# A convolutional FFN taken apart into two phases, its down-projection done as seven products

## The chip, the core and the metric

The kernel runs on one core of a Trainium2 chip. It computes one whole decoder layer in one launch. The metric is the device time of one execution in microseconds (us), as the median of several runs; lower is better. The engines are named as in the profile: PE does the matmuls (PEld loads their weights), DVE, ACT and POOL do the elementwise work, SP issues most of the DMAs. PE writes its results into eight PSUM banks of 128x512 numbers; everything else in the kernel's pools lies in SBUF.

## The reference, cut to what matters

Of the layer only its last part is touched: a gated feed-forward network with a causal convolution of width 3 over the tokens, on 1024 tokens, 1024 model columns and `D_FF` = 2816 hidden columns.

```
def conv_ffn(h, w_up, conv_w, conv_b, w_down):
    a, b = jnp.split(h @ w_up, 2, axis=-1)
    a = lax.conv_general_dilated(a, conv_w..., padding=[(CONV_WIDTH - 1, 0)], feature_group_count=D_FF) + conv_b
    return (jax.nn.gelu(a) * b) @ w_down
...
        x = x + merged @ w_o[l]
        x = x + conv_ffn(rms_norm(x, norm2_g[l]), w_up[l], conv_w[l], conv_b[l], w_down[l])
    return rms_norm(x, final_g)
```

## The kernel before, in words

Every product of two float32 numbers is made from three matmuls (`mm3`, L280 to L285): each operand is split into a high part `hi` that the PE's format holds and a low part `lo` = operand - `hi`, and hi·hi, hi·lo and lo·hi are added in PSUM. So an operand costs a cast on ACT, a subtraction on POOL or DVE, and three matmuls wherever it is used.

The 2816 hidden columns are handled as `NF` = 22 blocks of 128. The residual `x1`, 1024 tokens by 1024 columns, stays in SBUF, and the normalised input of the FFN lies there as seven prepared operands `B` (`B11`, `B21`, `B22` and the sums `T1` to `T4`, split into `hi` and `lo`, printed as `blk`).

`ffn` (L1357) is a generator that is entered twice. The first entry, in the middle of the output projection, loads and prepares the four operands of block 0. The second does the rest. For each block `j`:

- **Up-projection.** The two slices of `w_up` (for `a` and for `b`, each 1024x128, 512 KB) come in by two DMAs (L1370) into raw buffers (`wr` and `fr`, a ring of three). From them `prep` (L1374) makes the seven left operands of a seven-product scheme (Winograd's form of Strassen), `PRODUCTS`: the sums S1 to S4 on POOL (L1387 to L1394), the cast on ACT (L1398), the low part on POOL (L1399). `prep` is called three products ahead. A product is 4 x 3 = 12 matmuls of 128x512, into one PSUM bank, and is read out by ACT (L1500) or DVE (L1498, an add). Block 0 has eight products in four plus two groups, block 1 takes its seven in another order (`EARLY`).
- **Gate.** `conv` (L1437) and `gated` (L1452): the convolution of `a` over the tokens, gelu, times `b`, and the split of the gated activations of the first and second half of the tokens into `hi` and `lo`.
- **Down-projection of block j-1.** The rows of `w_down` of that block come in by two DMAs of 256 KB (L1404) and are split (`prep_down`, L1406 on ACT, L1407 on POOL). Then `down` (L1410) makes 16 tiles, 8 of tokens by 2 halves of the output columns, 3 matmuls each, into the PSUM bank printed as `T`, and DVE adds each to `x1` (L1419). They stand between the products: two or three tiles behind each.

After the loop the last two blocks' down-projections are made together, 16 tiles of 6 matmuls, and behind each pair of tiles the final normalisation of a tile of tokens: `squares` (L1547, ACT) and `finish` (L1553, DVE and POOL, and two stores to `out` of 256 KB, L1565).

The order on each engine is that of the program text, apart from what the scheduler of the framework moves; each engine goes through its instructions in order and waits for the semaphores of each, and SP also issues DMAs in order. An order is shown below with the change.

Of the kernel before, what the change touches and what calls it, by code (L numbers as in the profile page):

```python
# [13 lines left out]
P = 128  # L14
S = 1024
# [215 lines left out]
class Trunk:  # L231
# [1125 lines left out]
    def ffn(self, np_, x1, B):  # L1357
        nc, a, wp = self.nc, self.a, self.wp
        wup, wdn = a["w_up"][0], a["w_down"][0]
        raws, ops, wds, gs = {}, {}, {}, {}  # L1360
        cnt = {"raw": 0, "op": 0}
        last = NF - 1

        def load(j):
            pair = []
            for c0 in (j * P, DFF + j * P):
                pool, tag = (fp, "fr") if cnt["raw"] % 3 == 2 else (wp, "wr")
                cnt["raw"] += 1
                r = pool.tile([P, 8, P], F32, tag)
                nc.sync.dma_start(r, wup[:, c0:c0 + P].rearrange("(k p) n -> p k n", p=P))  # L1370
                pair.append(r)
            q = {"A11": pair[0][:, 0:4], "A12": pair[0][:, 4:8], "A21": pair[1][:, 0:4], "A22": pair[1][:, 4:8]}
            raws[j] = q

        def prep(j, i):

            if j > last:
                return
            if i == 0 and 0 < j < last:
                load(j + 1)  # L1380
            q = raws[j]
            name = (("A11", "A12", "A21", "A22") if j == 0 else [x for x, _ in (self.EARLY if j == 1 else self.PRODUCTS)])[i]
            g = nc.gpsimd.tensor_tensor
            e = g if j > 1 else nc.vector.tensor_tensor
            if name == ("S1" if j == 1 else "S2"):
# [13 lines left out]
            g(o[:, 1], q[name], o[:, 0].bitcast(F32), ALU.subtract)  # L1399
            ops[j, i] = o  # L1400

        def prep_down(j, n):
            raw = np_.tile([P, 512], F32, "tt")
            nc.sync.dma_start(raw, wdn[j * P:(j + 1) * P, n * 512:n * 512 + 512])  # L1404
            w = np_.tile([P, 2, 512], F32R, "t2") if j < last else wp.tile([P, 2, 512], F32R, ("wh", "wl")[n])
            nc.scalar.copy(w[:, 0], raw)  # L1406
            nc.gpsimd.tensor_tensor(w[:, 1], raw, w[:, 0].bitcast(F32), ALU.subtract)  # L1407
            wds[j, n] = w

        def down(j, t, n, tag="T"):  # L1410
            gh, gl = gs[j][t // 4]
            ts = slice((t % 4) * P, (t % 4) * P + P)
            ps = self.psA.tile([P, 512], F32, tag)
            if j == last:
                h0, l0 = gs[j - 1][t // 4]
                self.mm3(ps, (h0[:, ts], l0[:, ts]), (wds[j - 1, n][:, 0], wds[j - 1, n][:, 1]), True, False)
            self.mm3(ps, (gh[:, ts], gl[:, ts]), (wds[j, n][:, 0], wds[j, n][:, 1]), j != last, True)
            cs = slice(n * 512, n * 512 + 512)
            nc.vector.tensor_tensor(x1[:, t, cs], ps, x1[:, t, cs], ALU.add)  # L1419

        load(0)
        seq = [(0, i) for i in range(4)] + [(j, i) for j in range(1, NF) for i in range(7)]
# [3 lines left out]
        fp = Pool(self, "ffn", {"t1": 2, "sv": 2, "fst": 4})  # L1426
        load(1)
        AHEAD = 3
        todo = []
        for j in range(NF):  # L1430
            cw = [self.ccols[:, x * NF + j:x * NF + j + 1] for x in range(4)]
            sv = fp.tile([P, 2], F32, "sv")
            p1 = fp.tile([P, 512], F32, "p1")
            u2 = fp.tile([P, 512], F32, "u2")
            u3 = fp.tile([P, 512], F32, "u3")
            gs[j] = []

            def conv(hh, src):
                t1 = fp.tile([P, 512], F32, "t1")
                nc.scalar.activation(t1, src, AF.Identity, scale=cw[2], bias=cw[3])  # L1440
                for sh in (1, 2):
                    nc.vector.scalar_tensor_tensor(t1[:, sh:512], src[:, 0:512 - sh], cw[2 - sh], t1[:, sh:512],  # L1442
                                                   ALU.mult, ALU.add)
                if hh == 0:
                    nc.vector.tensor_copy(sv, src[:, 510:512])
                else:
                    nc.vector.scalar_tensor_tensor(t1[:, 0:1], sv[:, 1:2], cw[1], t1[:, 0:1], ALU.mult, ALU.add)
                    nc.vector.scalar_tensor_tensor(t1[:, 0:2], sv, cw[0], t1[:, 0:2], ALU.mult, ALU.add)
                nc.scalar.activation(t1, t1, AF.Gelu_apprx_tanh)
                gs[j].append(t1)  # L1450

            def gated(hh, b):  # L1452
                t1 = gs[j][hh]
                pool, tag = (wp, "wr") if (j, hh) == (last, 1) else (np_, ("x", "x", "gb")[(2 * j + hh) % 3])
                g = pool.tile([P, 2, 512], F32R, tag)
                gh, gl = g[:, 0], g[:, 1]
                nc.vector.tensor_tensor(t1, t1, b, ALU.mult)
                nc.scalar.copy(gh, t1)
                nc.vector.tensor_tensor(gl, t1, gh.bitcast(F32), ALU.subtract)
                gs[j][hh] = (gh, gl)  # L1460

            if j == 0:
                su = fp.tile([P, 512], F32, "su")
                for gi, grp in enumerate(((("A11", "B11"),), (("A12", "B21"),), (("A21", "B11"),), (("A22", "B21"),),
                                         (("A11", "T1"), ("A12", "B22")), (("A21", "T1"), ("A22", "B22")))):
                    ps = self.psA.tile([P, 512], F32, ("dn", "S", "S", "dn", "S")[gi % 5])
# [5 lines left out]
                    if gi % 2 == 0 and gi < 4:  # L1472
                        nc.scalar.copy((p1, u2)[gi // 2], ps)
                        continue
                    d, s = ((u3, p1), (su, u2), (p1, p1), (u2, u2))[(0, 0, 0, 1, 2, 3)[gi]]
# [223 lines left out]
```

## Time and profile before

| | |
|---|---|
| median of 3 runs | 1813.07 us (1812.57 to 1818.72) |
| the profiled execution | 1815.99 us, its span 1814.2 us, mean granted PE clock 0.985 |
| busy, share of the span | PE 96%, PEld 79%, DVE 68%, ACT 41%, POOL 32% |
| HBM read, written | 146.86 MB, 48.64 MB |

The stages by the times at which their instructions run: projections and the three attention mixers to about 880 us, merge 905 to 1008, output projection 1009 to 1108, FFN matmuls 1113 to 1803, and the last normalisation to the end of the span. The profile is of one execution: "span" is from its first to its last instruction, and its own time is a little longer. A row of the timeline has the start, the duration, the engine, the line, the operation and the tiles, and in brackets how long the engine had been idle and what ended that. A row of windows has for each engine the busy time and the count of instructions in a stretch of time, then the granted PE clock, the DMA engines' share and GB/s.

### The profile page before, as it was taken

The page shows a single profiled execution, that of the slowest core. Times are in us where ns is not written, and L with a number is a line of the kernel's source. Part 1 is how long each engine was busy: PE and PEld are TensorE (multiplying, and loading weights), DVE is VectorE, ACT ScalarE, POOL GpSimd, SP SyncE. Part 2 cuts the span into 40 slices and gives each one's busy share as a digit, 9 for nine tenths or more (in the row PEclk, how much of TensorE's full clock was granted, in tenths as well). Part 3 has the DMA queues.
Part 4 walks back from the last instruction along what each step waited for, and adds up shares of the span by engine and source line. Part 5 has one row for each costly group of instructions (what it writes and reads, how often), then busy time and mean ns, then how long its engine had stood idle before and what let it go on. Part 6 is the DMA issues. An engine that isn't in the chain of part 4 may idle for free.

```text
span 1814.2 us, 24514 instructions
## 1 busy us (share of the span) xinstructions
PE 1737.0 (96%) x8732; PEld 1425.5 (79%) x8732; DVE 1231.5 (68%) x2659; ACT 746.6 (41%) x1557; POOL 579.8 (32%) x435
## 2 busy tenths in 40 slices
PE   7999999879899999999999999899999999999997
PEld 6887887768687888888877887678878777877776
DVE  7366677646467775666567349877777777777777
ACT  5334555533354544555554224433333233333334
POOL 4311101002111111111134305555555555555561
PEclk9999999989899999999999999899999999999999
DMA  8756566677525264311466600121111111111112
GB/s 254 211 137 162 140 166 165 174 202 183 134 74 143 78 159 119 89 59 52 140 205 197 209 0 18 41 64 41 54 52 53 53 53 53 53 47 53 52 36 110
DMA packets 191648, 194.39 MB, mean 107 GB/s; under 512 B 16200, under 2 KB 155566, under 8 KB 191318
## 3 DMA queue, kind: packets, MB, share of 16 engines
q1 hardware_dynamic: 182870, 174.84, 34.3%
q10 hardware_dynamic: 8208, 15.21, 2.3%
q0 software_dynamic: 448, 2.78, 0.5%
q8 instruction: 69, 1.13, 0.3%
q14 instruction: 53, 0.43, 0.1%
HBM read 146.86 MB, written 48.64 MB: 108 GB/s over the span
## 4 chain that ended last, share of the span: by engine, by line
PE 52%; DVE 5%; DMA 2%; POOL 1%; ACT 1%; issue 1%; DVEq 0%; SPq 0%; ACTq 0%; POOLq 0%
PE dn L285 7%; PE dn L283 7%; PE dn L284 7%; PE S L285 5%; PE S L283 5%; PE S L284 5%; PE T L283 4%; PE T L285 4%; PE T L284 4%; PE T L769 1%; DVE t L1442 1%; DVE x L1419 1%; PE S L701 1%; PE PV L799 1%; DMA wr<-w_o 1%
## 5 line engine op out<-in xcount | busy, mean ns | idle before, releaser
L271 POOL TENSOR_TENSOR wl<-wr,wh 128x1024 fp32r<-128x1024 f32 (+2 forms) x60 | 113.4, 1890 | 696.6 <-ACT wh L269 605.5
L283 PE MATMUL dn<-hTh,wh 128*128 128x512 f32 x704 | 285.9, 406 | 2.0 <-DVE sl L488 2.0
L285 PE MATMUL dn<-hTh,wl 128*128 128x512 f32 x704 | 278.3, 395 | 0.0
L284 PE MATMUL dn<-hTl,wh 128*128 128x512 f32 x704 | 277.6, 394 | 0.0
L1419 DVE TENSOR_TENSOR x<-T,x 128x512 f32<-128x512 f32 x326 | 221.3, 686 | 9.9 <-PE T L285 9.4
L712 ACT ACTIVATE p<-S,sm 128x384 f32<-128x384 f32 (+2 forms) x192 | 106.5, 559 | 138.7 <-DVE sm L708 103.1
L285 PEld LDWEIGHTS dn<-hTh,wl 128*128 128x128 f32 x704 | 133.4, 190 | 29.2
L283 PEld LDWEIGHTS dn<-hTh,wh 128*128 128x128 f32 x704 | 134.3, 191 | 20.8 <-DVE sl L488 2.4
L284 PEld LDWEIGHTS dn<-hTl,wh 128*128 128x128 f32 x704 | 134.1, 191 | 19.1
L776 DVE TENSOR_TENSOR tl<-T,th 128x512 fp32r<-128x512 f32 (+2 forms) x202 | 115.4, 585 | 33.3 <-ACT th L775 32.3
L704 DVE TENSOR_REDUCE sm<-S 128x1 f32<-128x384 f32 (+2 forms) x192 | 96.3, 525 | 54.5 <-PE S L701 53.3
L775 ACT CAST th<-T 128x512 fp32r<-128x512 f32 (+2 forms) x202 | 99.7, 510 | 66.5 <-PE T L769 64.1
L701 PE MATMUL S<-k,q 114*128 114x384 f32 (+6 forms) x240 | 95.9, 400 | 16.0 <-issue 8.0
L798 PE MATMUL PV<-th,v 128*128 128x256 f32 (+1 forms) x362 | 93.9, 284 | 3.4 <-DVE yt L815 2.9
L769 PE MATMUL T<-ident,p 128*128 128x128 f32 x610 | 93.4, 275 | 2.1 <-DVE tl L776 2.1
L799 PE MATMUL PV<-tl,v 128*128 128x256 f32 (+1 forms) x362 | 89.2, 283 | 2.3 <-DVE tl L776 2.3
L283 PE MATMUL T<-t,x 128*128 128x512 f32 x219 | 89.9, 410 | 0.8 <-DVE x L1419 0.6
L697 PE MATMUL S<-k,q 128*128 128x384 f32 (+2 forms) x240 | 84.3, 351 | 6.5 <-DMA k<-dk_b 4.9
L285 PE MATMUL T<-t,x 128*128 128x512 f32 x219 | 86.2, 394 | 0.0
L284 PE MATMUL T<-t,x 128*128 128x512 f32 x219 | 85.6, 391 | 0.0
L769 PEld LDWEIGHTS T<-ident,p 128*128 128x128 f32 x610 | 72.6, 141 | 14.6 <-DVE tl L776 3.1
L798 PEld LDWEIGHTS PV<-th,v 128*128 128x128 f32 x362 | 69.1, 191 | 8.6 <-DVE yt L815 5.2
(481 smaller groups left out, 4494.1 us busy)
## 6 DMA issues: line engine op xcount, KB each, us to landing
wr<-w_in SPq DMA_DIRECT2D x44, 512.0 KB
wr<-w_up SPq DMA_DIRECT2D x30, 512.0 KB
dg<-f ACTq DMA_DIRECT2D x48, 256.0 KB
gr<-dg SPq DMA_DIRECT2D x24, 512.0 KB
tt<-w_down SPq DMA_DIRECT2D x44, 256.0 KB
x<-x SPq DMA_DIRECT2D x16, 512.0 KB
fr<-w_up SPq DMA_DIRECT2D x14, 512.0 KB
q<-dq_c SPq DMA_DIRECT2D x12, 512.0 KB
```

Source lines behind the costliest of these rows:

```text
L271: eng.tensor_tensor(lo, raw, hi.bitcast(F32), ALU.subtract)
L283: nc.tensor.matmul(out, st[0], mv[0], start=first, stop=False)
L284: nc.tensor.matmul(out, st[0], mv[1], start=False, stop=False)
L285: nc.tensor.matmul(out, st[1], mv[0], start=False, stop=last)
L701: nc.tensor.matmul(ps[:, 0:wn * P], q[1][0:R, qs], k[1][0:R, cs], start=False, stop=True)
L712: nc.scalar.activation(pt[:, 0:m, :].rearrange("p a b -> p (a b)"), v, AF.Exp, bias=mx, accum_out=sm[:, 2 + ci:3 + ci])
L769: nc.tensor.transpose(ps[:, n * P:(n + 1) * P], b, self.ident)
L775: nc.scalar.copy(th[:, cs], ps[:, cs])
L776: nc.vector.tensor_tensor(tl[:, cs], ps[:, cs], th[:, cs].bitcast(F32), ALU.subtract)
L798: nc.tensor.matmul(unit.pv[:, oc], w, th[:, cs], start=first and i == 0, stop=False)
L799: nc.tensor.matmul(unit.pv[:, oc], w, tl[:, cs], start=False, stop=e)
L1419: nc.vector.tensor_tensor(x1[:, t, cs], ps, x1[:, t, cs], ALU.add)
```

## The change

The FFN becomes two phases, with DRAM between them.

**Phase 1** makes only the up-projections and gates. The blocks are taken in the order 0, 11, 1, 12, ..., 10, 21. The gated activations are not split; as soon as the two blocks k and k+11 are there, they are the left operands of a second seven-product scheme: `sums` makes their four sums on DVE, and seven tiles of 256 KB are stored to DRAM (`dl[k]`). In the same phase `down_weights(k)` loads the two matching row blocks of `w_down` (512 KB each), makes the four sums T1 to T4 on POOL and stores them to DRAM (`dt[k]`, 2 x 512 KB); it is called in every second block. The low parts of the up-projection's operands (from the third block on) move from POOL to DVE. The convolution of the second half of the tokens reads its two halo columns from a buffer of 514 columns, which takes the place of two small fix-up instructions. The products rotate over all eight PSUM banks.

**Phase 2**, `ffn_down`, multiplies halves of the tokens (2 x 512), of the contraction (2 x 11 blocks) and of the outputs (2 x 512) in seven products. Six of them go over 11 operand pairs each: load the left and the right tile (two DMAs of 256 KB), one cast on ACT and one subtraction on DVE of 128x1024, then 4 tiles of tokens x 3 matmuls of 128x512, accumulated over the 11 pairs in four PSUM banks. The operands have a ring of five buffers and are asked for four ahead. The seventh product's eleven operands are prepared during the first six, one at every sixth step, and kept. The results are added to `x1` and to two helper sums `U` and `V`, and the last normalisation of the first four token tiles stands behind the fifth product, that of the other four behind each tile of the seventh.

The core of the diff (the block loop's bookkeeping and block 1's own order are left out):

```diff
+    DOWN = (("A11", "B11"), ("A12", "B21"), ("S2", "T2"), ("S1", "T1"), ("S4", "B22"), ("S3", "T3"), ("A22", "T4"))
...
+        order = [j for k in range(NH) for j in (k, k + NH)]
...
-            g(o[:, 1], q[name], o[:, 0].bitcast(F32), ALU.subtract)
-        def prep_down(j, n):
...
-        def down(j, t, n, tag="T"):
...
+            (v if s > 1 else g)(o[:, 1], q[name], o[:, 0].bitcast(F32), ALU.subtract)
+        def down_weights(k):
+            w = [np_.tile([P, 2, 512], F32, "t2") for _ in range(2)]
+            for x in range(2):
+                r = (k + x * NH) * P
+                nc.sync.dma_start(w[x], wdn[r:r + P].rearrange("p (n c) -> p n c", n=2))
+            g(w[0][:, 1], w[0][:, 1], w[0][:, 0], ALU.subtract)
+            g(w[1][:, 1], w[1][:, 1], w[0][:, 1], ALU.subtract)
+            g(w[0][:, 0], w[1][:, 1], w[0][:, 0], ALU.subtract)
+            g(w[1][:, 0], w[1][:, 0], w[1][:, 1], ALU.subtract)
+            for x in range(2):
+                nc.sync.dma_start(dt[k][:, 2 * x:2 * x + 2], w[x])
+        def left(k, name, src):
+            nc.sync.dma_start(dl[k][:, self.LEFT.index(name)], src)
+        def sums(k):
+            ga, gb = gs[k], gs[k + NH]
+            s1 = np_.tile([P, 512], F32, "tt")
+            v(s1, ga[:, 1], gb[:, 1], ALU.add)
+            left(k, "S1", s1)
+            v(ga[:, 1], ga[:, 0], ga[:, 1], ALU.subtract)
+            v(ga[:, 0], s1, ga[:, 0], ALU.subtract)
+            nc.sync.dma_start(dl[k][:, 0:2], ga)
+            v(gb[:, 0], gb[:, 0], ga[:, 0], ALU.subtract)
+            left(k, "S4", gb[:, 0])
...
+                if s > 1 and s % 2 == 0 and i == 2:
+                    sums(s // 2 - 1)
+                if s % 2 == 1 and i == 4:
+                    down_weights(s // 2)
+                ps = self.bank_tile()
...
-                for _ in range((0, 0, 0, 0, 5, 5, 6)[i] if j == 1 else ((i + 1) * 16) // 7 - (i * 16) // 7):
-                    if todo and j < last:
-                        down(*todo.pop(0))
...
+        def operands(p, k, keep=None):
+            an, bn = self.DOWN[p]
+            pool = ring()
+            raw = pool.tile([P, 2, 512], F32, "wr")
+            nc.sync.dma_start(raw[:, 0], dl[k][:, self.LEFT.index(an)])
...
+            nc.sync.dma_start(raw[:, 1], src)
+            hi, lo = ((keep or pool).tile([P, 2, 512], F32R, n) for n in (("hi", "lo") if keep else ("wh", "wl")))
+            nc.scalar.copy(hi, raw)
+            v(lo, raw, hi.bitcast(F32), ALU.subtract)
+            return hi, lo
+        def step(ps, op, t, first, last):
+            (hi, lo), ts = op, slice(t * P, t * P + P)
+            self.mm3(ps, (hi[:, 0, ts], lo[:, 0, ts]), (hi[:, 1], lo[:, 1]), first, last)
...
+        for p in range(6):
+            ps = [self.bank_tile() for _ in range(4)]
+            for k in range(NH):
+                n = p * NH + k
+                if n + AHEAD < len(seq):
+                    ops[n + AHEAD] = operands(*seq[n + AHEAD])
+                if n % 6 == 5:
+                    lasts.append(operands(6, len(lasts), rp))
+                o = ops.pop(n)
+                for t in range(4):
+                    step(ps[t], o, t, k == 0, k == NH - 1)
```

The orders below list instructions as line, operation, result and inputs, with the line numbers of the kernel that they come from; the numbers behind a tile's name tell buffers apart.

On POOL, early in phase 1. Before, a block's rows are the up-projection's sums (L1387 to L1394), its low parts (L1399) and the two low parts of `w_down` (L1407, `t<-tt`):

```order
L1394 TENSOR_TENSOR wr_12824<-wr_12824 128x512
L1399 TENSOR_TENSOR wh_13187<-wr_12826,wh_13187 128x512
L1407 TENSOR_TENSOR t_2636_13219<-tt_13217,t_2636_13219 128x512
L1399 TENSOR_TENSOR wl_13214<-wr_12826,wl_13214 128x512
L1399 TENSOR_TENSOR wh_13246<-su_13103,wh_13246 128x512
L1387 TENSOR_TENSOR su_13347<-wr_13070 128x512
L1389 TENSOR_TENSOR wr_13070<-fr_13068,wr_13070 128x512
L1399 TENSOR_TENSOR wl_13280<-wr_12824,wl_13280 128x512
L1399 TENSOR_TENSOR wh_13316<-fr_13068,wh_13316 128x512
L1391 TENSOR_TENSOR fr_13068<-su_13347,fr_13068 128x512
```

After, the four sums of `down_weights` (L1421 to L1424, one pair of `w_down` row blocks to each four rows), here of the eighth and ninth pair, and behind them the up-projection's sums of the seventh block (L1400 to L1407):

```order
L1421 TENSOR_TENSOR t_2778_14250<-t_2778_14250 128x512
L1422 TENSOR_TENSOR t_2779_14251<-t_2779_14251,t_2778_14250 128x512
L1423 TENSOR_TENSOR t_2778_14250<-t_2779_14251,t_2778_14250 128x512
L1424 TENSOR_TENSOR t_2779_14251<-t_2779_14251 128x512
L1421 TENSOR_TENSOR t_2827_14563<-t_2827_14563 128x512
L1422 TENSOR_TENSOR t_2828_14564<-t_2828_14564,t_2827_14563 128x512
L1423 TENSOR_TENSOR t_2827_14563<-t_2828_14564,t_2827_14563 128x512
L1424 TENSOR_TENSOR t_2828_14564<-t_2828_14564 128x512
L1400 TENSOR_TENSOR su_12711<-wr_12533 128x512
L1402 TENSOR_TENSOR wr_12533<-wr_12531,wr_12533 128x512
L1404 TENSOR_TENSOR wr_12531<-su_12711,wr_12531 128x512
L1407 TENSOR_TENSOR wr_12531<-wr_12531 128x512
```

The low parts have left POOL, and the scheduler has moved the sums of `w_down` forward: the program text calls the eighth pair in the sixteenth block, and it stands ahead of the seventh block's own sums. Each pair goes through the same two buffers `t2`, so its load waits until the pair before it is stored.

On DVE, in the middle of the block loop. Before, between the read-outs (L1498), the gate's products (L1457, L1459) and the convolution (L1442), stand the adds into the residual (L1419):

```order
L1498 TENSOR_TENSOR u_2809_14162<-dn_14259,u_2808_14161 128x512
L1419 TENSOR_TENSOR x_2293_11019<-T_14273,x_2293_11019 128x512
L1419 TENSOR_TENSOR x_2293_11019<-T_14278,x_2293_11019 128x512
L1419 TENSOR_TENSOR x_2293_11019<-T_14283,x_2293_11019 128x512
L1498 TENSOR_TENSOR p_2807_14160<-S_14295,u_2809_14162 128x512
L1419 TENSOR_TENSOR x_2293_11019<-T_14313,x_2293_11019 128x512
L1457 TENSOR_TENSOR t_2822_14239<-t_2822_14239,p_2807_14160 128x512
L1419 TENSOR_TENSOR x_2293_11019<-T_14318,x_2293_11019 128x512
L1459 TENSOR_TENSOR gb_14309<-t_2822_14239,gb_14309 128x512
```

After, the low parts of the up-projection's operands (L1412) stand between the read-outs (L1516), the convolution (L1470) and the gate (L1475):

```order
L1516 TENSOR_TENSOR u_2642_13385<-dn_13456,u_2641_13384 128x512
L1412 TENSOR_TENSOR wh_13474<-wr_13304,wh_13474 128x512
L1516 TENSOR_TENSOR p_2640_13383<-S_13477,u_2642_13385 128x512
L1475 TENSOR_TENSOR x_13386<-t_2651_13446,p_2640_13383 128x512
L1412 TENSOR_TENSOR wl_13497<-wr_13304,wl_13497 128x512
L1516 TENSOR_TENSOR u_2641_13384<-T_13500,u_2641_13384 128x512
L1516 TENSOR_TENSOR u_2642_13385<-T_13500,u_2642_13385 128x512
L1412 TENSOR_TENSOR wh_13515<-wr_13304,wh_13515 128x512
L1516 TENSOR_TENSOR u_2641_13384<-S_13518,u_2641_13384 128x512
L1412 TENSOR_TENSOR wl_13542<-fr_13306,wl_13542 128x512
```

The sixteen adds of a block are gone, and seven low parts have come.

On SP, from the end of the block loop. Before, there are the last loads of `w_down`, the load of `final_g` and the stores of the result:

```order
L1404 DMA tt_16863<-w_down 128x512
L1404 DMA tt_16981<-w_down 128x512
L1404 DMA tt_16986<-w_down 128x512
L1543 DMA wr_16991<-final_g 128x1024
L1565 DMA out<-wh_17035 128x512
```

After, at the change of phase: loads of phase 2's operands (L1584 the left, L1590 the right tile; `wr_15262` is the first operand, `wr_15269` the second, `wr_15276` the third, `wr_15313` the sixth, `wr_15332` the seventh, `wr_15396` the first of the last product, `wr_15415` the eleventh), with the stores of the last pair's activations (L1430 and L1440) among them. The rows follow each other, in two pieces:

```order
L1584 DMA wr_15262<-dl_2334_11495 128x512
L1590 DMA wr_15262<-w_down 128x512
L1584 DMA wr_15269<-dl_2335_11496 128x512
L1590 DMA wr_15269<-w_down 128x512
L1430 DMA dl_2344_11505<-x_15102 128x512
L1584 DMA wr_15313<-dl_2339_11500 128x512
L1590 DMA wr_15313<-w_down 128x512
L1572 DMA fg_15260<-final_g 128x1024
L1584 DMA wr_15332<-dl_2340_11501 128x512
L1590 DMA wr_15332<-w_down 128x512
L1584 DMA wr_15396<-dl_2334_11495 128x512
L1430 DMA dl_2344_11505<-x_15102 128x512
```

```order
L1430 DMA dl_2344_11505<-tt_15240 128x512
L1590 DMA wr_15396<-dt_2345_11506 128x512
L1584 DMA wr_15415<-dl_2344_11505 128x512
L1440 DMA dl_2344_11505<-gb_14951 128x1024
L1430 DMA dl_2344_11505<-x_15102 128x512
L1590 DMA wr_15415<-w_down 128x512
L1584 DMA wr_15491<-dl_2337_11498 128x512
L1590 DMA wr_15491<-w_down 128x512
L1584 DMA wr_15276<-dl_2336_11497 128x512
L1590 DMA wr_15276<-w_down 128x512
```

The third operand's two loads stand behind those of the sixth, the seventh, the eleventh, the fifteenth and the last product's first, and behind all of the last pair's stores.

More of the change, by code (lines that the diff above doesn't have):

```diff
@@ L1371, in load, with names, prep @@
                 pair.append(r)
[L1372 to L1385, printed above, removed]
+            raws[s] = {"A11": pair[0][:, 0:4], "A12": pair[0][:, 4:8], "A21": pair[1][:, 0:4], "A22": pair[1][:, 4:8]}
+        def names(s):
+            return ("A11", "A12", "A21", "A22") if s == 0 else [x for x, _ in (self.EARLY if s == 1 else self.PRODUCTS)]
+        def prep(s, i):
+            if i == 0 and 0 < s < NF - 1:
+                load(s + 1)
+            q = raws[s]
+            name = names(s)[i]
+            e = g if s > 1 else v
+            if name == ("S1" if s == 1 else "S2"):
                 s1 = fp.tile([P, 4, P], F32, "su")
@@ L1421, in ffn @@
         load(0)
-        seq = [(0, i) for i in range(4)] + [(j, i) for j in range(1, NF) for i in range(7)]
+        seq = [(0, i) for i in range(4)] + [(s, i) for s in range(1, NF) for i in range(7)]
         for x in range(4):
@@ L1425, in ffn @@
         yield
[L1426 removed]
+        fp = Pool(self, "ffn", {"t1": 2})
         load(1)
         AHEAD = 3
[L1429 to L1430 removed]
+        for s in range(NF):
+            j = order[s]
             cw = [self.ccols[:, x * NF + j:x * NF + j + 1] for x in range(4)]
[L1432 removed]
             p1 = fp.tile([P, 512], F32, "p1")
[L1434 removed]
+            u2h = fp.tile([P, 514], F32, "u2")
+            u2 = u2h[:, 2:514]
             u3 = fp.tile([P, 512], F32, "u3")
[L1436 removed]
+            gs[j] = np_.tile([P, 2, 512], F32, ("x", "x", "gb")[s % 3])
+            ts = {}
             def conv(hh, src):
@@ L1565, in finish @@
                 (nc.sync, nc.scalar)[n].dma_start(a["out"][0, t * P:(t + 1) * P, cs], o[:, cs])
-        for t in range(NT):
-            for n in range(2):
-                down(last, t, n, ("T", "S", "dn")[(2 * t + n) % 3])
-            squares(t)
-            if t:
-                finish(t - 1)
-        finish(NT - 1)
-        fp.close()
+        seq = [(p, k) for p in range(6) for k in range(NH)]
+        AHEAD = 4
+        ops = {n: operands(*seq[n]) for n in range(AHEAD)}
+        lasts = []
+        lo_, hi_ = slice(0, 512), slice(512, 1024)
+        for p in range(6):
[9 more added lines that the diff above has]
+                    step(ps[t], o, t, k == 0, k == NH - 1)
+            for t in range(4):
+                add = lambda d, r: v(d, ps[t], r, ALU.add)
+                c11, c12 = x1[:, t, lo_], x1[:, t, hi_]
+                c21, c22 = x1[:, t + 4, lo_], x1[:, t + 4, hi_]
+                if p == 0:
+                    nc.scalar.copy(U[:, t], ps[t])
+                    add(c11, c11)
+                elif p == 1:
+                    add(c11, c11)
+                elif p == 2:
+                    add(U[:, t], U[:, t])
+                elif p == 3:
+                    add(V[:, t], U[:, t])
+                    v(c12, c12, V[:, t], ALU.add)
+                    v(c21, c21, U[:, t], ALU.add)
+                    v(c22, c22, V[:, t], ALU.add)
+                elif p == 4:
+                    add(c12, c12)
+                    squares(t)
+                    finish(t)
+                else:
+                    add(c22, c22)
+                    add(c21, c21)
+                    squares(t + 4, (1,))
+        for t in range(4, 8):
+            ps = self.bank_tile()
+            for k in range(NH):
+                step(ps, lasts[k], t - 4, k == 0, k == NH - 1)
+            v(x1[:, t, lo_], ps, x1[:, t, lo_], ALU.add)
+            squares(t, (0,))
+            finish(t)
+        rp.close()
+        dp.close()
     def run(self):
```

171 lines of the change are left out of this document (87 added, 84 removed).

## The prediction

> **What bounds the kernel now.** I read the page first, then the windows of the FFN, the waits of PE, and last the timeline at the places that the change touches. From the page, the span and the busy time of each engine:
>
> ```profile
> span 1814.2 us, 24514 instructions
> PE 1737.0 (96%) x8732; PEld 1425.5 (79%) x8732; DVE 1231.5 (68%) x2659; ACT 746.6 (41%) x1557; POOL 579.8 (32%) x435
> ```
>
> The share of PE says little by itself, so the windows: the block loop, the last products, the last down-projections, then two stretches ahead of the FFN that are busy with DMA (columns: stretch, PE, PEld, DVE, ACT, POOL busy with counts, granted clock, DMA share, GB/s).
>
> ```profile
> 1300.00:1340.00 40.00, 39.91 (x173) 31.95 (x172) 30.52 (x45) 13.06 (x22) 21.19 (x16) 1.00 0.20 59
> 1783.00:1803.00 20.00, 20.00 (x89) 16.35 (x88) 18.87 (x51) 14.10 (x38) 3.89 (x3) 1.00 0.27 100
> 1000.00:1020.00 20.00, 20.00 (x90) 16.51 (x89) 9.26 (x14) 4.87 (x7) 5.88 (x3) 1.00 0.71 264
> 0.00:45.00 45.00, 31.96 (x230) 30.83 (x231) 33.72 (x85) 25.79 (x54) 19.79 (x31) 1.00 0.81 255
> ```
>
> And all waits of PE from 1185 to 1770 us (total, times, longest):
>
> ```profile
> PE T L283 <- DVE x L1419: 0.6, 3, 0.2
> ```
>
> In the FFN PE never waits, at the full clock. So a matmul removed there is time removed, as long as PE goes on not waiting; and each wait that the change brings costs its length.
>
> **What a matmul costs.** One product of the loop in the same place of two successive blocks, twelve matmuls of a product, and twelve of the last down-projections (ends of the stretches):
>
> ```profile
> 1302.56 0.57 ACT L1500 COPY p<-S 128x512 f32<-128x512 f32 x1
> 1333.49 0.57 ACT L1500 COPY p<-S 128x512 f32<-128x512 f32 x1
> ...
> 1770.00 0.40 PE L283 MATMUL dn<-blk,wl 128*128 128x512 f32 x1
> 1772.80 0.40 PE L283 MATMUL S<-blk,wh 128*128 128x512 f32 x1
> ...
> 1785.54 0.39 PE L284 MATMUL T<-t,x 128*128 128x512 f32 x1
> 1788.26 0.39 PE L284 MATMUL dn<-t,x 128*128 128x512 f32 x1
> ```
>
> A block has 84 + 48 = 132 matmuls in 30.93 us, 0.2343 each; products alone take 2.80/12 = 0.2333, down-projections alone 2.72/12 = 0.2267.
>
> **Removed.** The down-projection falls from 22 x 16 x 3 = 1056 matmuls to 7 x 11 x 4 x 3 = 924: 132 fewer, at 0.2343 a gain of 30.9 us if PE stays as full as now. The rest is what PE then waits for. The 352 adds into x1 on DVE, 44 casts and 44 low parts of w_down go too; they lay beside PE (no wait above names them but for 0.6 us), worth nothing by themselves. ACT only gets less to do in phase 1: two casts of the gate and two of w_down a block go, and a copy of two columns comes.
>
> **Start of phase 1.**
>
> ```profile
> 1133.54 0.39 PE L285 MATMUL S<-blk,wh 128*128 128x512 f32 x1
> 1138.84 0.68 PE L283 MATMUL dn<-blk,wl 128*128 128x512 f32 x1 [4.91 <-DVE su L1476]
> 1139.31 0.63 PE L284 MATMUL dn<-blk,wl 128*128 128x512 f32 x1
> 1142.57 0.39 PE L283 MATMUL dn<-blk,wl 128*128 128x512 f32 x1
> ...
> 1133.92 1.31 POOL L1399 TENSOR_TENSOR wl<-fr,wl 128x512 fp32r<-128x512 f32 x1
> ...
> 1135.30 0.54 DVE L1349 TENSOR_TENSOR x<-t,blk 128x128 f32<-128x128 f32 x1
> ...
> 928.01 0.44 SPq L1272 DMA_DIRECT2D gr<-dg  x1
> 932.05 1.06 ACT L1273 ACTIVATE gr<-gr 128x1024 f32<-128x1024 f32 x1 [1.57 <-DMA gr<-dg]
> ...
> 1177.52 0.59 ACT L1500 COPY p<-S 128x512 f32<-128x512 f32 x1 [0.30 <-PE S L285]
> ```
>
> Today PE stops here for 4.91 us for a full bank, which eight banks would take away. But POOL's order now has the first pair's four ops ahead of the low part at 1133.92, and these need a t2 buffer that DVE reads until 1135.84. The 512 KB load (4.04 us, the gr rows; 0.44 to issue) lands at 1140.3; three ops and the low part, 4 x 1.31, end at 1145.5, with semaphores 1145.9. So PE idles 12 us, and it restarts slowly: after 4.91 us idle, matmuls came every 0.43 us until 1142.57, 1.7 us lost over nine. The 84 matmuls left of the second block and the third block's first product: 1145.9 + 1.7 + 84 x 0.2333 = 1167.2, where 1177.5 stands now with down-projections already in it. Were the load 3 us earlier or 5 later: −3 to +5.
>
> **The rest of PE's work.** Phase 1 has 96 + 21 x 84 = 1860 matmuls, of which 1668 are left: x 0.2333 = 389.1. Phase 2: 924 x 0.2267 = 209.5; at the loop's 0.2343, 216.5. I take the first: down-projections alone are the like case.
>
> **Elementwise work in phase 1.** Durations (shortest, median, longest ns, or count, busy us and mean):
>
> ```profile
> L1399 POOL TENSOR_TENSOR wh<-wr,wh x44: 1285/1298/1752, 1033.9 to 1771.0; 128x512 fp32r<-128x512 f32 x44
> L1498 DVE TENSOR_TENSOR u<-S,u x48: 674/688/693, 1191.3 to 1780.3; 128x512 f32<-128x512 f32 x48
> L1459 DVE TENSOR_TENSOR x<-t,x x29: 674/693/1775, 1141.3 to 1779.1; 128x512 fp32r<-128x512 f32 x29
> L1442 DVE SCALAR_TENSOR_TENSOR t<-u,ccols,t x46: 741/743/1844, 1130.9 to 1784.2; 128x511 f32<-128x511 f32 x23, 128x510 f32<-128x510 f32 x23
> L1457 DVE TENSOR_TENSOR t<-t,p x21: 676/1317/1786, 1175.8 to 1776.6; 128x512 f32<-128x512 f32 x21
> ...
> 1413.12 1.30 POOL L1399 TENSOR_TENSOR wh<-fr,wh 128x512 fp32r<-128x512 f32 x1 [0.29 <-ACT wh L1398]
> 1413.67 1.30 DVE L1457 TENSOR_TENSOR t<-t,p 128x512 f32<-128x512 f32 x1
> ```
>
> A block lasts 84 x 0.2333 = 19.6 us. DVE has seven PSUM adds (4.8), seven low parts (4.8), four of the convolution (3.0), two gates (1.4) and half of `sums` (1.4): 15.4, so it fits. POOL has the four up-projection sums, 5.2. The last pair of rows shows the danger: a DVE op with both inputs in SBUF took 1.30 us beside a POOL op, where 0.68 is the shortest. Such DVE ops make 10.6 us a block, with POOL's 5.2 it is 15.8 of 19.6: it fits even one after the other.
>
> *Early blocks.* All eleven pairs of `down_weights` stand within the first seven blocks or so on POOL, each behind the store of the one before. Load and store:
>
> ```profile
> 1189.28 0.37 SPq L1370 DMA_DIRECT2D wr<-w_up  x1
> 1193.21 1.32 POOL L1387 TENSOR_TENSOR su<-wr 128x512 f32<-128x512 f32 x1 [3.96 <-DMA wr<-w_up]
> ...
> 1811.28 0.34 ACTq L1565 DMA_DIRECT2D out<-wl  x1
> ```
>
> The last store, 256 KB, took 1814.2 − 1811.28 = 2.9 us; a 512 KB store isn't shown, I take the load's 3.9. A pair then takes 2.6 to 3.9 us of POOL, 3.9 stored, 4.0 to 4.9 loaded: about 12.3 to 14.3. The seventh block's sums stand behind nine pairs; seven cycles lie between the third block's sums and these, and PE wants them 4.2 blocks apart, 83 us. So they come 7 x 12.3 − 83 = 3 us, to 17 us, late. The lateness is not paid twice by later blocks. I take 8 (0 to 17), nearer the shorter cycle, since load and store of the two buffers overlap partly.
>
> *SP* gets 10 to 14 DMAs for two blocks where it had 8; at 0.34 to 0.44 us of issue each that is up to 6 of 39 us, hidden unless one waits with others behind it, which is the case at the change of phase.
>
> *Later blocks.* Three raw buffers go round by S4's low part, load 4.0 to 4.9, three sums 3.9, cast and low part: 12.9 to 15.2 us against five products, 14.0. I take 4 in all (0 to 15).
>
> **Change of phase.** PE has two operands ahead, 24 matmuls, 5.6 us. The third's loads stand on SP behind loads into buffers that must be prepared first (sixth, seventh, the first of the last product), and behind the last pair's stores of `sums`.
>
> ```profile
> L269 ACT CAST wh<-wr 128x1024 fp32r<-128x1024 f32 x36 | 37.9, 1053 | 34.4 <-PE dn L284 29.3 <-issue 4.5 <-DMA wr<-w_in 0.6
> L1262 DVE TENSOR_TENSOR yl<-gr,yh x8: 1214/1226/1493, 892.3 to 909.1; 128x1024 fp32r<-128x1024 f32 x8
> ```
>
> From the end of phase 1: the first buffers go round, low part of the sixth operand at 5.2, stores, of the seventh at 8.6, S2/S3 at 10, of the last product's first at 12.4, third's loads issued at about 13.5, landed at 16.5 (3 us, from the 2.9 above), cast 1.05, low part 1.23: 18.9. PE waits 18.9 − 5.6 = 13.3, then slowly for 1.6: 14.9. If every DMA takes 2 us only, 10; if each takes the 4.9 us, 20.
>
> **Phase 2.** An operand is 12 matmuls, 2.72 us, with the last product's 2.3 in mean. ACT 1.05 and DVE 1.23 fit; 512 KB in 2.3 to 2.4 us is about 220 GB/s, and the windows show 255 and 264 with PE full. The `finish` of four tiles takes buffers of the same ring. I take 3 (0 to 5).
>
> **End.** Now from the last matmul to the end:
>
> ```profile
> 1802.77 0.39 PE L285 MATMUL T<-wl,wr 128*128 128x512 f32 x1
> ```
>
> 1814.2 − 1803.0 = 11.2, because eight `finish` have piled up on DVE. After, one is left behind eleven steps of 0.7 us: add 0.69, square 0.63, small ops about 2, scaling 1.4, store 2.9: 7.6.
>
> **Sum.** 1167.2 + 389.1 + 8 + 4 + 14.9 + 209.5 + 3 + 7.6 = 1803.3 us of span, 10.9 less. The profiled execution took 1.8 more than its span, and lay 2.9 above the median 1813.07. So 1803.3 + 1.8 − 2.9 = 1802.2. Half a per cent, about what a measurement of this kernel can tell from no change, is 1804.0 and 1822.1.
>
> **Rivals.**
>
> A. The forecast, 1794 to 1811. Chance 0.45, 0.30 of it below 1804.
>
> B. The waits are mostly hidden: pairs of `down_weights` cycle faster than the products need, and the third operand comes about as soon as phase 1 ends. For it: SP has little to do (the DMA share is 0.20 in the loop's window), so nothing but the order delays these. Without the 8, the 4 and half of the 14.9: 1783; with the rest gone too, 1772. Chance 0.20.
>
> C. The other side. DVE's SBUF ops and POOL's run one after the other in the early blocks. There `down_weights` gives POOL 44 / 7 = 6.3 more ops a block: 5.2 + 8.2 = 13.4, with DVE's 10.6 it is 24 against 19.6, and over seven blocks 4.3 x 7 = 30 in place of 8: 1824. It decides once the sum passes 19.6, that is from three more POOL ops a block. For it: the pair of rows at 1413. Against it: L1442's median stays 743 ns beside a POOL busy half the time. Chance 0.12.
>
> The Trainium skill, "SBUF — State Buffer", section "Who interferes with whom", says that a DVE instruction with two SBUF inputs contends with a GpSimd one that reads SBUF; by "two separate sides" the pair of ports is an exclusive lock. The pair at 1413 agrees with the first: 1.30 for 0.68. By the lock the time is C's.
>
> D. The raw buffers set the pace in all blocks: 15.2 against 14.0, 1.2 x 20 = 24 in place of 4: 1822. Against it: today the same ring feeds PE, though a block then has 30.9 us. Chance 0.08.
>
> E. The change does what it says, but the change of phase takes 20 and the early blocks 17: 1802 + 5 + 9 = 1816. Chance 0.15, of it 0.02 over 1822.
>
> So faster 0.30 + 0.20 = 0.50, same 0.15 + 0.13 = 0.28, slower 0.12 + 0.08 + 0.02 = 0.22. The range takes in B and half of C, 1781 to 1825; A's own is 1794 to 1811.
>
> **What would show it.** 132 fewer matmul rows of L283 to L285; one PE gap of about 12 us at 1134; waits for POOL's sums (L1400 to L1404) in blocks four to eight, none later than 1 us; one gap of 10 to 20 us between the phases; matmuls 0.227 apart after it with no wait for casts or low parts; 7 to 8 us after the last matmul. I am wrong if phase 2 waits for its operands at every step, if raw buffers hold up each block, or if the gap between the phases is missing.

## The result, and the profile after

The changed kernel takes 1839.2 us (median of 4 runs, 1838.91 to 1841.05) against 1812.8 us for the kernel before: a ratio of 1.0141, 95% interval 1.0118 to 1.0164. It is slower by 26 us where 11 us less were forecast. Its profiled execution has a span of 1839.3 us.

The page of the changed kernel: PE has 132 matmuls fewer and is busy for 26 us less, but the span grew by 25.

```profile
span 1839.3 us, 24513 instructions
PE 1711.3 (93%) x8600; PEld 1406.3 (76%) x8600; DVE 1205.0 (66%) x2518; ACT 770.8 (42%) x1572; POOL 397.0 (22%) x295
```

Windows of the changed kernel (columns as before): three stretches of the early blocks, one of the late blocks, the change of phase, and phase 2.

```profile
1133.00:1173.00 40.00, 31.50 (x123) 24.44 (x122) 29.42 (x33) 14.17 (x25) 32.31 (x24) 0.87 0.42 151
1173.00:1193.00 20.00, 13.61 (x58) 10.49 (x57) 12.68 (x16) 4.05 (x8) 7.94 (x7) 0.92 0.74 249
1233.00:1253.00 20.00, 10.52 (x34) 7.80 (x33) 11.23 (x13) 3.58 (x6) 11.80 (x9) 0.74 0.56 186
1533.00:1573.00 40.00, 39.85 (x171) 31.62 (x170) 31.90 (x46) 14.37 (x26) 10.57 (x8) 1.00 0.28 93
1599.00:1639.00 40.00, 22.86 (x91) 17.98 (x90) 18.77 (x19) 13.44 (x14) 0.00 (x0) 0.79 0.69 223
1653.00:1693.00 40.00, 40.00 (x178) 33.15 (x177) 23.39 (x22) 17.54 (x20) 0.00 (x0) 1.00 0.69 220
```

PE is full in the late blocks and in phase 2, and far from it in the early blocks and between the phases; there the granted clock falls too. The longest waits of PE from 1150 to 1300 us:

```profile
PE S L283 <- ACT wl L1411: 8.3, 1, 8.3
PE T L283 <- ACT wl L1411: 5.8, 1, 5.8
PE T L283 <- ACT wh L1411: 4.9, 1, 4.9
```

The marks that divide the span by the terms of the forecast, from the timeline: the third block's first product begins, its second begins (so twelve matmuls took 2.75 us), the tenth block's first product begins, phase 2 begins, the second operand ends, the third begins, the last matmul.

```profile
1163.91 0.39 PE L283 MATMUL T<-blk,wl 128*128 128x512 f32 x1
...
1166.66 0.39 PE L283 MATMUL S<-blk,wh 128*128 128x512 f32 x1
...
1334.86 0.39 PE L283 MATMUL S<-blk,wh 128*128 128x512 f32 x1
...
1599.42 0.39 PE L283 MATMUL S<-wh 128*128 128x512 f32 x1
...
1604.66 0.39 PE L285 MATMUL dn<-wh,wl 128*128 128x512 f32 x1
1622.14 0.79 PE L283 MATMUL S<-wh 128*128 128x512 f32 x1 [17.09 <-ACT wh L1592]
...
1831.24 0.39 PE L285 MATMUL dn<-hi,lo 128*128 128x512 f32 x1
```

| term | forecast, us | measured, us |
|---|---|---|
| end of the third block's first product | 1167.2 | 1166.7 |
| lost in the early blocks (between the first products of the third and the tenth block, beyond 7 x 84 x 0.2333 = 137.2) | 8 | 34 |
| lost in the later blocks (from there to 1599, beyond 1080 x 0.2333) | 4 | 10 |
| change of phase, idle and slow restart | 14.9 | 19 (17.2 idle) |
| phase 2, beyond 924 x 0.2267 = 209.5 | 3 | 3.5 |
| from the last matmul to the end | 7.6 | 7.8 |

So one term holds 26 of the 36 us by which the span missed. Between its marks PE idles for 25 us in eleven waits of over 0.3 us; the rest is that matmuls come slower behind a long wait: after the one of 8.3 us, twelve took 5.1 us. (The expectations of experiments 1 and 2 speak of 31 us ahead of the ninth block. That came from the read-out of the tenth block's first product at 1343.48, which ACT made 5.9 us after the product had ended.) The question for the experiments: what costs 34 us in the early blocks, where the eleven pairs of `down_weights` go through POOL?

One of those waits, the longest, from the timeline of the changed kernel:

```profile
1227.08 0.93 SPq L1430 DMA_DIRECT2D dl<-tt  x1
...
1230.01 0.68 DVE L1412 TENSOR_TENSOR wl<-fr,wl 128x512 fp32r<-128x512 f32 x1
...
1230.61 2.62 DVE L1470 SCALAR_TENSOR_TENSOR t<-p,ccols,t 128x511 f32<-128x511 f32 x2
1231.40 1.29 POOL L1422 TENSOR_TENSOR t<-t,t 128x512 f32<-128x512 f32 x1 [1.86 <-DMA t<-w_down]
...
1234.34 1.74 POOL L1424 TENSOR_TENSOR t<-t 128x512 f32<-128x512 f32 x1
1234.41 0.33 SPq L1426 DMA_DIRECT2D dt<-t  x1
...
1235.25 0.79 SPq L1384 DMA_DIRECT2D fr<-w_up  x1
...
1241.24 1.26 POOL L1400 TENSOR_TENSOR su<-fr 128x512 f32<-128x512 f32 x1 [5.17 <-DMA fr<-w_up]
...
1243.93 1.26 POOL L1404 TENSOR_TENSOR wr<-su,wr 128x512 f32<-128x512 f32 x1
1245.22 0.62 ACT L1411 CAST wl<-wr 128x512 fp32r<-128x512 f32 x1 [11.26 <-POOL wr L1404]
```

The product that PE waits for needs a sum that needs a slice of w_up. The buffer `fr` was free when its last reader ended, at 1230.69, but SP stood from 1228.0 at a pair's store, which waited for the pair's third sum on POOL; so the load went out at 1235.25 only, and took 6 us to land. DVE is late in the same stretch too: two convolution steps take 2.62 us beside a pair's POOL operations, where each takes 0.74 alone. From this alone, the order on SP, the load of the DMA and a conflict between DVE and POOL cannot be told apart.

### The profile page after: what moved, and what is told of

Same layout as the page of the kernel before. It is cut to its first block, busy times and chain, and to the rows that moved or that the text cites. A ratio compares the mean times of both kernels' runs of the same rounds, so it can differ in the third digit from the quotient of the medians.

```text
span 1839.3 us, 24513 instructions
## 1 busy us (share of the span) xinstructions
PE 1711.3 (93%) x8600; PEld 1406.3 (76%) x8600; DVE 1205.0 (66%) x2518; ACT 770.8 (42%) x1572; POOL 397.0 (22%) x295
## 5 line engine op out<-in xcount | busy, mean ns | idle before, releaser
L1593 DVE TENSOR_TENSOR wl<-wr,wh 128x1024 fp32r<-128x1024 f32 x66 | 80.2, 1223 | 63.0 <-ACT wh L1592 60.7
L1592 ACT CAST wh<-wr 128x1024 fp32r<-128x1024 f32 x66 | 69.3, 1053 | 95.8 <-PE dn L285 61.9
L799 PEld LDWEIGHTS PV<-tl,v 128*128 128x128 f32 x362 | 69.6, 192 | 6.2 <-DVE tl L776 3.7
L283 PE MATMUL S<-blk,wl 128*128 128x512 f32 x152 | 62.0, 408 | 12.2 <-ACT wl L1411 12.2
```

The lines of the kernel that those rows point to most:

```text
L283: nc.tensor.matmul(out, st[0], mv[0], start=first, stop=False)
L799: nc.tensor.matmul(unit.pv[:, oc], w, tl[:, cs], start=False, stop=e)
```

## Experiments

Times of kernels with one run are of that run; the kernel before took 1815.2, 1813.0 and 1814.9 us (medians) beside the three groups of runs.

**1. The pairs spread over the blocks.** POOL's order only:

```diff
 def prep(s, i):
-                e(q["A12"], q["A12"], q["S2"], ALU.subtract)
+                n = e(q["A12"], q["A12"], q["S2"], ALU.subtract)
...
+                if s > 1:
+                    mark[0] = n.ins
...
                 if s % 2 == 1 and i == 4:
-                    down_weights(s // 2)
+                    with self.tc.issue_after(mark[0]):
+                        down_weights(s // 2)
```

> The changed kernel with one edit: each pair's four sums of w_down on POOL are queued behind the up-projection's last POOL operation of the block in which the program text calls them, so one pair goes with every second block instead of eleven with the first seven. All theories explain the 31 us that phase 1 lost ahead of its ninth block by the crowd of pairs; theory T (order): the loads of w_up on SP and the sums of the up-projection on POOL stand behind a pair's stores and sums, which themselves wait for a DMA. Theory P (the shared port of DVE and POOL): pairs and DVE's operations run one after the other. Theory M (DMA): the loads of w_up take longer to land while the pairs' traffic runs. All three expect the loss to fall to a few us with the crowd gone: 1839 - 25 = 1814, 1808 to 1820. A fourth, N: the raw buffers' round and DVE's new low parts set the early blocks, whatever the pairs do: 1835 to 1840.

Measured: 1865.1 us, ratio to the kernel before 1.0288 (1.0266 to 1.031). All four theories are wrong here: spread out, the pairs cost more. From the sixth block to the last (the read-outs of their first products, 16 blocks on) a block takes 23.2 us:

```profile
1234.88 0.57 ACT L1524 COPY p<-T 128x512 f32<-128x512 f32 x1
...
1605.40 0.56 ACT L1524 COPY p<-T 128x512 f32<-128x512 f32 x1
```

That is 3.6 us above the 19.6 that the prediction gives its matmuls (the shortest blocks of these runs take 19.2). Against the kernel without pairs (experiment 2) it is (1865.1 − 1798.0) / 11 = 6 us for each pair, so what costs is not the crowd but each pair by itself. A stretch of the timeline shows how:

```profile
1421.70 3.48 DVE L1475 SCALAR_TENSOR_TENSOR t<-u,ccols,t 128x512 f32<-128x512 f32 x2
1423.00 1.63 POOL L1427 TENSOR_TENSOR t<-t,t 128x512 f32<-128x512 f32 x1
...
1426.31 1.73 POOL L1429 TENSOR_TENSOR t<-t 128x512 f32<-128x512 f32 x1
...
1426.81 1.77 DVE L1415 TENSOR_TENSOR wh<-wr,wh 128x512 fp32r<-128x512 f32 x1
...
1430.30 0.68 DVE L1415 TENSOR_TENSOR wh<-fr,wh 128x512 fp32r<-128x512 f32 x1
...
1431.66 0.39 SPq L1385 DMA_DIRECT2D fr<-w_up  x1
...
1438.14 1.30 POOL L1401 TENSOR_TENSOR su<-fr 128x512 f32<-128x512 f32 x1 [10.11 <-DMA dl<-x]
...
1442.82 0.80 PE L283 MATMUL T<-blk,wh 128*128 128x512 f32 x1 [3.38 <-ACT wh L1414]
```

While POOL works on a pair, two convolution steps take 3.48 us in place of 1.49, and a low part 1.77 in place of 0.69. So the low part behind these, the last reader of the raw buffer `fr`, runs at 1430.30 only; the next slice of w_up is loaded into `fr` behind it, the sum that reads it starts 6.5 us later, at 1438.14 (the row names a store that ended at about the same time), and then come the cast and the product. Part of the 6.5 us is the load itself, which took 3.9 in the kernel before (from 1189.28 to 1193.21).

**2 to 4. Without the pairs, and with either half of their work.**

```diff
 2:  -                if s % 2 == 1 and i == 4:
     -                    down_weights(s // 2)
 3:  one load of w[0], w[1] in all, no stores;
     +                if i == 4 and s <= 6:
     +                    with self.tc.issue_after(mark[0]):
     +                        for _ in range(1 if s == 1 else 2):
     +                            down_weights(0)
 4:  -            g(w[0][:, 1], w[0][:, 1], w[0][:, 0], ALU.subtract)
     ...
     -            g(w[1][:, 0], w[1][:, 0], w[1][:, 1], ALU.subtract)
```

> Leaves out down_weights altogether, loads, sums and stores; phase 2 reads all its right tiles from w_down instead (same sizes and count). T, P and M: the blocks come every 19.6 us from the third on but for some 6 us in later blocks, so about 1839 - 31 = 1808, 1803 to 1812. N: 1835 to 1840.

> The pairs' 44 POOL sums stay in the first seven blocks (one pair in the second, two in each of the next five), on two buffers that are loaded once, each group queued behind the up-projection's last POOL operation of its block; the pairs' loads and stores are left out, and phase 2 reads its right tiles from w_down. P: as late as the changed kernel, 1832 to 1840, since POOL and DVE do the same work in these blocks. T and M: as without pairs, 1805 to 1814.

> Leaves out the pairs' 44 POOL sums alone (the weights are stored to DRAM as they came); loads, stores and their place among SP's DMAs stay as the scheduler puts them. M: the loads of w_up land as late as before, 1830 to 1840. P: 1805 to 1814. T: the stores wait for a load only and POOL holds nothing up, so most of the loss goes: 1810 to 1822.

Measured: 1798.0 us without the pairs, 1835.7 with the POOL sums alone, 1810.6 with the loads and stores alone. So the pairs cost 41 us; POOL's part by itself costs 38, the DMA's part by itself 13, and they overlap. The first is 5 us below the expected range. Theory P holds in 3 and 4, T fails in 3 (4 lies at the lower end of its range), M fails in both. So the POOL sums are enough for the loss, without a single store on SP. How much of it goes by SP's order in the changed kernel, where the stores wait for these sums, was not measured. And 3 leaves two readings: that DVE and POOL hold each other up, or simply that POOL is taken up when the up-projection's sums are due.

**5. Fills in place of the sums.** The kernel with POOL's part alone, and one edit:

```diff
-            g(w[0][:, 1], w[0][:, 1], w[0][:, 0], ALU.subtract)
-            ... (4)
+            for x in range(4):
+                nc.gpsimd.memset(w[x % 2], 0.5)
```

> The kernel with the pairs' POOL sums alone (loads and stores left out, 1835.7 us) with one edit: each of these 44 sums becomes a fill of 128x1024 with a constant, in the same places of POOL's queue; a fill writes and reads nothing. Theory P (port): a DVE operation with two inputs in SBUF and a POOL operation that reads SBUF run one after the other, and the lengthened low parts hold up the three raw buffers; then the fills cost nothing, about the 1798 us of the kernel without pairs, 1796 to 1808. Theory Q (queue): the up-projection's sums come late because POOL is taken up, whatever it does; then 1825 to 1838 if a fill lasts as long as a sum.

Measured: 1801.4 us. The groups from 1130 to 1340 us (POOL) and 1150 to 1300 us (DVE), first with sums, then with fills (count, busy us, mean ns):

```profile
L1429 POOL TENSOR_TENSOR t<-t 128x512 f32<-128x512 f32 x11 | 18.7, 1696 | 0.0
...
L1476 DVE SCALAR_TENSOR_TENSOR t<-u,ccols,t 128x512 f32<-128x512 f32 x12 | 16.8, 1397 | 0.3
L1415 DVE TENSOR_TENSOR wl<-wr,wl 128x512 fp32r<-128x512 f32 x11 | 12.3, 1119 | 9.5 <-ACT wl L1414 9.5
...
L1524 DVE TENSOR_TENSOR u<-S,u 128x512 f32<-128x512 f32 x7 | 4.6, 682 | 0.0
```

```profile
L1430 POOL MEMSET t<- 128x1024 f32 x44 | 39.8, 958 | 0.0
...
L1415 DVE TENSOR_TENSOR wl<-wr,wl 128x512 fp32r<-128x512 f32 x14 | 11.1, 796 | 10.7 <-ACT wl L1414 10.7
L1474 DVE SCALAR_TENSOR_TENSOR t<-u,ccols,t 128x512 f32<-128x512 f32 x14 | 10.5, 746 | 0.3
```

With 40 us of fills at the same places, DVE's convolution step is back at 746 ns, which is its mean in the kernel without pairs too, and the time is within 3.4 us of that kernel (single runs, on two chips whose kernels before differ by 2.2). A fill lasts 0.96 us, shorter than a sum's 1.30 alone, so Q's condition is not quite met. But if the loss went with POOL's time, 0.96/1.30 of the 38 us, some 28, would have stayed by a rough estimate, or 21 by the 1.70 that a pair's first sum took beside DVE. So nearly all of it is the contention, which lengthens the operations of both engines. Which operations suffer shows it too: the adds that read one operand from PSUM (L1524) stay at 682 ns among the same sums. The Trainium skill, "SBUF — State Buffer", section "Who interferes with whom", says just this: a DVE instruction with two SBUF inputs contends with a GpSimd instruction that reads SBUF, not with one that only writes it. The rows agree.

**6. The pairs on DVE.**

```diff
-            g(w[0][:, 1], w[0][:, 1], w[0][:, 0], ALU.subtract)
+            v(w[0][:, 1], w[0][:, 1], w[0][:, 0], ALU.subtract)
...
-                if s % 2 == 1 and i == 4:
-                    down_weights(s // 2)
+                if s == 1 and i == 6 or s > 1 and s % 2 == 1 and i == 4:
+                    with self.tc.issue_after(mark[0]):      # DVE's last low part
+                        down_weights(s // 2)
```

> The changed kernel with the pairs' four sums on DVE instead of POOL, one pair in every second block, queued behind the low part of the next block's first operand. P: no POOL operation runs against DVE but the up-projection's own, and DVE has 2.8 us more in two blocks of 39.2: 1800 to 1812. Q: 2.8 us in front of DVE's low parts for each of eleven pairs, on the way of the raw buffers: about 1798 + 31 = 1829, 1820 to 1840.

Measured: 1813.7 us, ratio 1.0005 (0.9991 to 1.0019): 25.5 us less than the changed kernel, though the busier of the two engines has got the work. The edit also spreads the pairs; against experiment 1, which spreads them on POOL, it is 51 us less. A little above P's range, and 6 below Q's.

**7. The change of phase.** Phase 2's extra ring buffers in other memory:

```diff
-        dp = Pool(self, "down", {"wr": 3, "wh": 3, "wl": 3, "st": 4})
-        rp = Pool(self, "downr", {"hi": NH, "lo": NH}, side="right")
+        dp = Pool(self, "down", {"wr": 3, "wh": 3, "wl": 3}, side="right")
+        rp = Pool(self, "downr", {"hi": NH, "lo": NH, "st": 4})
```

> The changed kernel with one edit: phase 2's three extra ring buffers are put where the up-projection's operands lay instead of where its gates lay, so the third operand's loads wait for the last up-projection matmul and no longer for the last stores; SP's order comes out by operand number. The theory that the gap between the phases (17.5 us and a slow restart) comes from the third operand's place on SP: the gap falls to 3 to 8 us, 1839 - 12 = 1827, 1823 to 1832. Rival: the loads need 6 us to land and the gap stays 10 or more whatever the order: 1833 to 1840.

Measured: 1819.6 us, ratio 1.0041 (1.0028 to 1.0053), 19.6 us less than the changed kernel. In the changed kernel the third operand's load, its cast and the restart stand so:

```profile
1614.65 0.38 SPq L1584 DMA_DIRECT2D wr<-dl  x1
...
1621.05 1.04 ACT L1592 CAST wh<-wr 128x1024 fp32r<-128x1024 f32 x1 [8.57 <-DMA wr<-w_down]
```

It was issued 15.2 us after phase 1 ended, and its two halves were there 6.4 us later. With the ring moved, the window across the change of phase is full:

```profile
1592.00:1632.00 40.00, 40.00 (x176) 32.65 (x175) 30.22 (x31) 22.98 (x25) 0.00 (x0) 1.00 0.91 304
```

The gap is not 3 to 8 us but gone, since the loads now start before the last products end.

**8. Both.** The edits of 6 and 7 in one kernel.

> Both edits of the two kernels before in one: pairs on DVE, ring moved. If their gains add up: 1790 to 1800, faster than the kernel before by about 1%. If phase 1 is bound elsewhere: 1810 to 1828.

Measured: 1794.3 us, ratio 0.9905 (0.9881 to 0.9929). The gains add up: 25.5 + 19.6 = 45.1, and the changed kernel's 1839.2 − 1794.3 = 44.9. This is faster than both kernels.

**9 and 10. A fourth raw buffer.** The pairs go through one of the two `t2` buffers in two halves of 256 columns; the other becomes a raw buffer. First with the pairs on POOL as in 1, then on top of 8:

```diff
-                pool, tag = (fp, "fr") if cnt["raw"] % 3 == 2 else (wp, "wr")
+                c = cnt["raw"] % 4 if cnt["raw"] > 3 else (1, 1, 2, 3)[cnt["raw"]]
+                pool, tag = (np_, "t2b") if c == 0 else (fp, "fr") if c == 2 else (wp, "wr")
```

> The kernel with the pairs spread over the blocks on POOL (1865 us) with a fourth raw buffer for w_up; to make room, a pair goes through one buffer in two halves of 256 columns. Theory R (round): the port holds up DVE's low parts, and it costs PE time because a raw buffer that comes free late delays the next load, so the next sums; with a fourth buffer the loads go out earlier and most of the 67 us above the kernel without pairs goes: 1805 to 1825. Rival S: PE waits for the late low parts themselves, buffers or not: 1845 to 1870.

> The kernel with pairs on DVE and the ring moved (1794 us) with the fourth raw buffer, pairs in halves. R: its blocks come every 20.4 us where 19.6 are needed, and the waits of 1 to 2.5 us for casts in every second block are the same round; they go: 1794 - 14 = 1780, 1776 to 1788. Rival: the waits have another cause: 1790 to 1798.

Measured: 1830.3 us with the pairs on POOL, 35 less than in 1 and 32 above the kernel without pairs, between the two expectations. So about half of a pair's price on POOL went by way of the raw buffers, if the halving of the pairs, which came with the fourth buffer, changed nothing by itself; that was not tested. In one place of the other half, at 1461, three operations of a pair, 2.2 us, stood on POOL between two of the up-projection's sums, and PE waited 1.7 us for the cast behind them. How the rest divides was not measured.

On top of 8: 1782.3 us, ratio 0.9814 (0.9792 to 0.9836), as R expected. The read-outs of the sixth and the last block's first products, of 8 and then with the fourth buffer:

```profile
1223.12 0.57 ACT L1522 COPY p<-T 128x512 f32<-128x512 f32 x1
...
1552.44 0.57 ACT L1522 COPY p<-T 128x512 f32<-128x512 f32 x1
```

```profile
1221.78 0.57 ACT L1524 COPY p<-T 128x512 f32<-128x512 f32 x1
...
1539.51 0.56 ACT L1524 COPY p<-T 128x512 f32<-128x512 f32 x1
```

20.6 us a block became 19.9; the shortest blocks take 19.2.

**11. The low parts back on POOL,** in the kernel of 8 (the pairs, on DVE, now queued behind the gate's product):

```diff
-            n = (v if s > 1 else g)(o[:, 1], q[name], o[:, 0].bitcast(F32), ALU.subtract)
+            n = g(o[:, 1], q[name], o[:, 0].bitcast(F32), ALU.subtract)
```

> The kernel with pairs on DVE and the ring moved (1794 us) with the up-projection's low parts back on POOL. Theory P (port): DVE operations with two inputs in SBUF, 7.2 us a block, and POOL's eleven operations, 14.3, run one after the other: 21.5 against the 19.6 us of a block, so at least 1.9 x 20 = 38 us more, 1825 to 1850. Rival: POOL at 14.3 us of 19.6 fits, as it does in the kernel before: 1790 to 1805.

Measured: 1827.9 us, 34 more. The block takes 22.3 us:

```profile
1227.66 0.56 ACT L1521 COPY p<-T 128x512 f32<-128x512 f32 x1
...
1584.35 0.57 ACT L1521 COPY p<-T 128x512 f32<-128x512 f32 x1
```

P's sum for one after the other was 21.5. So that part of the change is right: with the pairs on DVE, phase 1 is slower without it. (One run, and the pairs' place in DVE's order is another than in 8.)

## Why the prediction was wrong

*Early blocks: the step that failed.* I priced the crowd of pairs by its cycle of load, POOL and store against the time at which the seventh block's sums are due, at 8 us (0 to 17). Measured were 34, and 1 by the same marks without the pairs (experiment 2). What this leaves out is that a pair's POOL operations and DVE's operations with two SBUF inputs hold each other up: the pairs' sums alone cost 38 us (experiment 3), fills in their places 3 (experiment 5). I had the row for it (1.30 us for 0.68 at 1413) and made it rival C: 30 us in place of 8, 1824, chance 0.12. That was the right mechanism, and its 30 near the 34.

The cycle was mis-sized as well. Its terms as listed add up to 10.5 to 12.7 us, not 12.3 to 14.3, and in the changed kernel the pairs' first sums (L1421, from 1135.1 to 1297.0) came every 16.2 us. Seven such cycles would be 30 us late too, so its size alone does not rule the cycle out as the cause. Experiment 3 speaks against it: it has neither the loads nor the stores, and loses as much.

Two arguments against C misled me. The first was that L1442's median is 743 ns beside a busy POOL. A median of 46 hides the ones that met a POOL operation: its longest was 1844, and L1457, which did meet them, had a median of 1317 in the same fence. The second was the budget: I let contention cost only where DVE's and POOL's times add up to more than a block. With the pairs spread, 2 x 15.8 + 5.2 = 36.8 us are less than two blocks' 39.2, and each pair still cost 6 us, about half of it (experiment 9) because the delayed low parts free the raw buffers. I had that round as rival D, by itself, at 15.2 us against 14.0. Neither rival alone was the case; the two work in series, which I didn't consider.

*Start.* Right in the sum (1166.7 for 1167.2), for partly wrong reasons: the waits at the start were 1.87 and 4.98 us rather than 12 in all, but they began later and another, of 1.66, followed. The pairs cost here too: without them that product ends at 1158.9.

*Later blocks.* 10 us for 4. By the same marks it is 9 without the pairs (experiment 2) and 2 with the fourth raw buffer (experiment 10): here the raw buffers' round, rival D's mechanism, does cost something by itself, less than half of its 24. The range of that round, 12.9 to 15.2, can't be added up again from the prices shown.

*The rest of PE's work.* 0.2333 us a matmul was dear: most products of phase 1 take 2.75 us for twelve, some 2.80. At 2.75 the 389.1 would be 7 us less, and the early and later losses 36 and 14.

*Phase 2, end.* 3.5 and 7.8 us for 3 and 7.6. The bet on 0.2267 a matmul, and that the cast, the low part and the two loads of each operand hide behind 2.7 us of matmuls, held. Of the two windows that I named as busy with DMA and PE full, only the one at 1000 is: in the other, from 0 to 45, PE was busy for 31.96 us of 45.

*Change of phase.* The mechanism, the third operand behind other loads and stores on SP, is shown by experiment 7. The size: 19 for 14.9. The third operand's load went out 1.7 us later than the 13.5 that I took. I let it land in 3 us, from a store at the quiet end; with six others issued in the same 4 us its two halves took 6.4. And PE began behind the cast, without the low part's 1.2 us.

*The matmuls removed.* No run shows their worth apart from the waits. The best kernel, with both faults mended and a fourth buffer, takes 1782.3 us, 32.6 below the kernel before on the same chip, where the forecast's gross gain was 30.9; that the two are close is partly chance, since this kernel still waits in places and its end is some 3 us shorter.

## What to carry to other kernels

When work is moved between DVE and POOL, look first at which operations read two tensors from SBUF on DVE and which read SBUF on POOL: side by side each of them can take about 1.7 us here, where alone it is 0.7 and 1.3, and a median over a group hides it; compare shortest and longest. Then ask what a delayed operation frees: a ring of buffers with little slack can turn a delay of 2 to 3 us on DVE into as much idle PE time (3.4 us in experiment 1's stretch), before the two engines' times fill a block. At a change of phase, the memory that the next phase's first buffers take over, and what must be finished with it, decides how soon its loads can be queued.

## What the runs showed of the hardware

The fills on POOL did not lengthen DVE's convolution step (746 ns, the same as without them), while sums at the same places nearly doubled it (1397); in the prediction's budgets I had priced every POOL operation alike. DVE's adds with one operand in PSUM were never touched: in the changed kernel's early blocks, from 1167 to 1305 us, they took 676 to 692 ns. Nor do the two engines simply take turns: in the 3.48 us of experiment 1's two convolution steps POOL got about two sums done, where 2 x (0.75 + 1.30) = 4.1 us would go by one after the other, so the exclusive lock that the prediction names is not borne out in full. A wait of PE costs more than its length when a slow restart follows, and that came after short waits too, though not after each: after 1.88 us (at 1339.65) matmuls came every 0.43 us for about 3 us, after 1.66 us (at 1161.49) they were back at 0.23 with the second. And DMA traffic of 304 GB/s with the DMA engines 0.91 busy left PE full in the window of experiment 7, more than the 264 at 0.71 that I had used as a bound.
